# Two FFN gate-up passes: the weight sums of the block-product down are gathered in steps 2 to 7 of each group, and the small tables move to the four-tile part

## The chip, the cores and the metric

The kernel runs on one core of one Trainium2 chip. The metric is the device time of one execution in microseconds (us), the median of several runs. Beside it stands one execution that the hardware profiler recorded: its span (first to last instruction) and its trace. TensorE multiplies, VectorE (DVE) and ScalarE (ACT) do elementwise work, GpSimd (POOL) and SyncE (SP) mostly issue DMA transfers.

## The reference, cut to what matters

The input is 1,024 prompt rows and 128 sample rows of width 1,024, so nine tiles of 128 rows, through one layer: a SwiGLU feed-forward block, a mixer (window attention and a spatial gate), and a second SwiGLU block, each between RMS norms. What the change touches is

```python
def swiglu(x, w_gate, w_up, w_down):
    return (jax.nn.silu(x @ w_gate) * (x @ w_up)) @ w_down
x = x + 0.5 * rms_norm(swiglu(rms_norm(x, norm_g[0]), f1_g, f1_u, f1_d), norm_g[1])
...
x = x + 0.5 * rms_norm(swiglu(rms_norm(x, norm_g[4]), f2_g, f2_u, f2_d), norm_g[5])
```

with an inner width of 2,816, all in float32. The relative-bias table and the attention sinks, which the small tables below come from, are used only in the mixer.

## The kernel before, in words

**Exact products from halves.** Every operand is split into a rounded part and a rest (`hi` and `lo`; `wh`, `wl` for weights): ScalarE copies the rounded part (L158), VectorE subtracts (L161, "rest-cut" below). A product is three matmuls, `mm3`, at L306 to L308; the third is the first to need `wl`.

**Tiles and parts.** The nine row tiles are worked in two parts, five tiles (`parts1[0]`, then `parts2[0]` in the second block) and four tiles (`parts1[1]`, `parts2[1]`). Each part has a gate-up pass and a down pass. So the order is: five-tile gate-up, five-tile down, four-tile gate-up, four-tile down; the mixer; and the same four passes again.

**A gate-up pass** has eleven groups of 256 weight columns (`NG`). In a group the product is formed by seven block products instead of eight, in the order A11, S1, S2, S4, S3, A12, A22, for gate and up each. That makes fourteen steps; `drive` counts them through the whole pass and runs, before step i, the tasks listed under i. The first group of the first pass is plain and has 16 steps. The weight blocks S1 to S4 are sums that VectorE forms from raw weights (L200). In the rows S1 is `arena<-wr`, S2 `gn<-arena,wr`, S4 `arena<-wr,gn` and S3 `wr<-wr`. Behind the products VectorE adds results (L600) and multiplies gate by up (L658).

**The weight loads.** The raw weights lie in three buffers `wr`. A group takes two, raw 0 and raw 1, each of two transfers (gate and up, 512 KB each) that SP issues at L140. `fetch` issues the next load as soon as the buffer it needs is free. The buffer that the next group's raw 1 goes to is that of this group's raw 0, free when the rest-cut of S3 is done. The next group's S1 needs raw 1.

**The weight sums.** The five-tile down pass also uses block products, and four of its right-hand blocks (T1 to T4) are sums of the down weights. `down_sums` makes them during the five-tile gate-up: for each of eleven row blocks f, POOL loads two pieces of 512 KB into one of two places of `arena` (L232), VectorE does four subtractions of 128x512 (L239, "sums"), and POOL stores 1 MB to `t_d` (L241). A load into a place waits for the store out of it. `spread` places a task every so many steps; `in_order` ties its first ScalarE and VectorE instruction behind what was emitted before it on that engine. What is not tied, a scheduler places.

**The small tables.** `small_loads` clears five tiles on VectorE (L926) and loads tables with some twenty tiny transfers on POOL; two of them bring the sinks to `sink_p`, eight to `sink_s`. `small_turns` multiplies the bias table out on TensorE, negates the sinks on VectorE (`nsink_p`, `nsink_s`, L949), writes the bias spread `rb`, 1 MB, from POOL (L950), and turns a small weight matrix.

Of the kernel before, what the change touches and what calls it, by code (L numbers as in the profile page):

```python
# [32 lines left out]
NG = D_FF // 256  # L33
# [9 lines left out]
def tile_hybrid_layer(  # L43
# [38 lines left out]
    def tmp(n=BW):  # L82
        return fslot(F32, n)
# [40 lines left out]
    raws = {"n": 3}  # L124
# [118 lines left out]
        return ([lambda: load(0)] + [lambda f=f, i=i: make(f, i) for f in range(NG - 1) for i in range(4)] +  # L243
                [lambda: load(NG - 1)], [lambda i=i: make(NG - 1, i) for i in range(4)])

    def spread_sums(up, w_d, t_d, i):

        most, rest = down_sums(w_d, t_d)
        spread(up, most, i, (107 - i) / len(most))
        spread(up, rest, 114, 2)  # L250

    def plan_down(w_d, t_d):
        for _, right, _ in DOWN:
# [395 lines left out]
    def gate_up(part):  # L649

        w, gate = part.w, {}

        def done(g, m, c, j, v, in_place):
            if m == 0:
                t = gate[c, j] = v if in_place else tmp(w)
                nc.scalar.activation(out=t, in_=v, func=AF.Silu)  # L656
            else:
                nc.vector.tensor_tensor(out=part.g[2 * g + c][:, j * w:(j + 1) * w], in0=gate[c, j], in1=v,  # L658
                                        op=ALU.mult)

        return block_products(part, [part.order(g) for g in range(NG)], [2] * NG, done)
# [195 lines left out]
    def drive(gen, tasks):  # L857

        i = 0
        while True:  # L860
            for t in tasks.pop(i, ()):
                t()
            if next(gen, gen) is gen:
                break
            i += 1
        assert not tasks, sorted(tasks)

    def in_order(task):

        def f():  # L870
            seen = nc.cur_bb.bb.instructions
            n = len(seen)
            task()
            for eng in (mybir.EngineType.Activation, mybir.EngineType.DVE):
                mine = [i for i in seen[n:] if i.engine == eng]
                before = next((i for i in reversed(seen[:n]) if i.engine == eng), None)
                if mine and before is not None:
                    tc.add_manual_dep(mine[0], before.name, mybir.DependencyInfo(
                        mybir.DependencyClass.NoSync, mybir.DependencyReason.DATA), reason="in_order")
        return f  # L880

    def strict(task, engines=(mybir.EngineType.PE, mybir.EngineType.Activation, mybir.EngineType.DVE)):

        seen = nc.cur_bb.bb.instructions
        n = len(seen)
        task()
        for eng in engines:
            before = next((i for i in reversed(seen[:n]) if i.engine == eng), None)
            for i in [i for i in seen[n:] if i.engine == eng]:
                if before is not None:  # L890
                    tc.add_manual_dep(i, before.name, mybir.DependencyInfo(
                        mybir.DependencyClass.NoSync, mybir.DependencyReason.DATA), reason="strict")
                before = i

    def spread(tasks, todo, i, step):

        for t in todo:
            tasks.setdefault(int(i), []).append(in_order(t))
            i += step
# [59 lines left out]
    parts1 = [Part(TILES[0], 0, 5, True), Part(TILES[1], 0, 4)]  # L959
# [4 lines left out]
    t1_d, t2_d = (dram.tile([P, NG, 4, 512], F32, name=f"t{i}_d") for i in (1, 2))  # L964
# [78 lines left out]
    def next_tasks(part, src):  # L1043


        def begin():
            raws["n"] = 2

        def load():
            t = wr.tile([P, 2048], F32, tag="wr", name="wr")  # L1050
            for i, v in enumerate((place(0), gnp.tile([P, D], F32, tag="gn", name="gn"), t[:, :D], t[:, D:])):
                part.load(src, i, v)

        def end():
            raws["n"] = 3

        up, dn = {14 * (NG - 1) + (2 if src is x_in else 0): [begin]}, {90: [load]}
        n = norm_tasks(part.tiles, part.h)
        spread(dn, n[:part.n + 1], 103, 1.2)
        spread(dn, n[part.n + 1:], 111, 2)  # L1060
        spread(dn, part.operand_tasks()[0] + [end], 121, 4.4)
        return up, dn


    up, dn = next_tasks(parts1[1], x_in)
# [8 lines left out]
    up[2] = [lambda t=t: strict(t) for t in norm_tasks([3, 4], part.h, True, [nc.scalar, nc.vector])]  # L1074
    for i, t in zip((10, 11, 12, 13, 14, 16, 17, 19), part.sums()):
        up.setdefault(i, []).append(t)
    up.setdefault(14, []).append(lambda: strict(small_loads))
    spread(up, [small_turns], 45, 1)
    spread_sums(up, f1_d[0], t1_d, 15)
    drive(gate_up(parts1[0]), up)  # L1080
    drive(down_blocks(parts1[0]), dn)


    drive(gate_up(parts1[1]), {14 * (NG - 1): [lambda: raws.update(n=2)]})

# [700 lines left out]
    up, dn = next_tasks(parts2[1], x2_d)  # L1788
    spread(up, late, 0, 1.5)
    spread(up, [x2_inverse] + [lambda i=i: x2_put_last(i) for i in (3, 0, 1, 2)], 7, 2)  # L1790
    spread_sums(up, f2_d[0], t2_d, 22)
    drive(gate_up(parts2[0]), up)
    drive(down_blocks(parts2[0]), dn)

# [81 lines left out]
```

## Time and profile before

| what | us |
|---|---|
| median of 3 runs (lowest to highest) | 2560.33 (2557.41 to 2561.31) |
| the profiled execution | 2564.02 |
| its span | 2562.3 |
| PE busy | 2507.5 (98%) |
| DVE busy | 1996.2 (78%) |
| ACT busy | 1425.5 (56%) |
| mean granted clock of TensorE | 0.993 of full speed |

The profiled execution lies 3.69 us above the median. Some 55 us of the span are not covered by PE. A change of the order in which VectorE works can pay only in such gaps, in the time in which TensorE had the lower clock, or not at all. "A group" in the rows below is the time from one point of the pass to the same point of the next group: the moment at which the last S4 product is ready and VectorE adds it (called the mark).

### The profile page before, as it was taken

Reading aid. Unit: us, or ns where it says so; the run is one execution under the profiler, and the core shown is the slowest. Engines: PE = TensorE matmul, PEld = TensorE weight load, DVE = VectorE, ACT = ScalarE, POOL = GpSimd, SP = SyncE. Lnnn points to the kernel's source line nnn. Section 1 sums busy time; section 2 is a strip of 40 time slices with the busy share of each in tenths; the row PEclk is TensorE's granted clock in tenths of the full one; section 3 lists DMA queues with packets and bytes.
Section 4 is the critical chain, followed back from the end, with each engine's and each line's share of the span. In section 5 each row is a group of like instructions: output and inputs, shape, how many; then the busy total and the mean of one; then the engine's idle time right before and its main releaser. Section 6 shows DMA issues by size and latency. Waiting matters only on the chain.

```text
span 2562.3 us, 43644 instructions
## 1 busy us (share of the span) xinstructions
PE 2507.5 (98%) x16848; PEld 2352.5 (92%) x16848; DVE 1996.2 (78%) x3508; ACT 1425.5 (56%) x2692; POOL 236.8 (9%) x372
## 2 busy tenths in 40 slices
PE   9989999999999999999999999999999999999998
PEld 8989987999978999999989899997999987899986
DVE  7778777888877686787857877787887786888885
ACT  6434457555565555776446568646444456655552
POOL 1100000000110000011400101140001000000030
PEclk9999999999999999999999999999999999999999
DMA  5764344533443224424533344373566335533362
GB/s 157 203 209 158 105 158 161 164 115 116 144 165 105 83 79 137 146 78 146 181 111 93 128 149 128 98 257 103 181 214 213 121 126 173 178 116 116 125 205 83
DMA packets 243856, 366.89 MB, mean 143 GB/s; under 512 B 13640, under 2 KB 181040, under 8 KB 240832
## 3 DMA queue, kind: packets, MB, share of 16 engines
q1 hardware_dynamic: 192048, 229.66, 28.0%
q0 software_dynamic: 29344, 110.29, 13.1%
q10 hardware_dynamic: 22256, 24.15, 2.7%
q8 instruction: 132, 2.16, 0.4%
q14 instruction: 76, 0.62, 0.1%
HBM read 300.81 MB, written 63.18 MB: 142 GB/s over the span
## 4 chain that ended last, share of the span: by engine, by line
PE 81%; DVE 8%; DMA 6%; ACT 3%; issue 2%; ACTq 0%; POOL 0%; SPq 0%; DVEq 0%; POOLq 0%
PE ps L308 25%; PE ps L306 25%; PE ps L307 25%; DMA wr<-in_ffn_w_up_dram 3%; DVE wl L161 2%; PE ps L1486 2%; PE ps L487 1%; PE ps L1473 1%; PE ps L1438 1%; DVE arena L239 1%; ACT wh L158 1%; DMA wr<-in_w_in_dram 1%; DVE arena_r L317 0%; PE ps L1285 0%; DMA sink_p<-in_attn_sinks_dram 0%
## 5 line engine op out<-in xcount | busy, mean ns | idle before, releaser
L306 PE MATMUL ps<-arena_r,wh 128*128 128x320 f32 (+1 forms) x4160 | 1242.2, 299 | 15.7 <-DVE t L600 9.3
L308 PE MATMUL ps<-arena_r,wl 128*128 128x320 f32 (+1 forms) x4160 | 1228.6, 296 | 13.1 <-DVE wl L161 12.8
L307 PE MATMUL ps<-arena_r,wh 128*128 128x320 f32 (+1 forms) x4160 | 1228.9, 296 | 0.5 <-DVE arena_r L317 0.3
L306 PEld LDWEIGHTS ps<-arena_r,wh 128*128 128x128 f32 x4160 | 786.5, 189 | 19.8 <-issue 11.0
L308 PEld LDWEIGHTS ps<-arena_r,wl 128*128 128x128 f32 x4160 | 785.5, 189 | 17.1 <-DVE wl L161 16.8
L307 PEld LDWEIGHTS ps<-arena_r,wh 128*128 128x128 f32 x4160 | 787.0, 189 | 1.9 <-DVE arena_r L317 1.1
L161 DVE TENSOR_TENSOR wl<-wr,wh 128x1024 fp32r<-128x1024 f32 (+1 forms) x444 | 544.7, 1228 | 219.8 <-ACT wh L158 216.9
L158 ACT CAST wh<-wr 128x1024 fp32r<-128x1024 f32 (+1 forms) x444 | 455.2, 1026 | 210.2 <-PE ps L307 147.4
L306 PE MATMUL ps<-wh,arena_r 128*128 128x512 f32 x892 | 358.6, 402 | 2.9 <-ACT arena_r L316 2.9
L308 PE MATMUL ps<-wh,arena_r 128*128 128x512 f32 x892 | 353.9, 398 | 1.8 <-DVE arena_r L317 1.8
L307 PE MATMUL ps<-wl,arena_r 128*128 128x512 f32 x892 | 352.5, 395 | 1.3 <-DVE wl L161 1.3
L316 ACT CAST arena_r<-arena 128x512 fp32r<-128x512 f32 (+4 forms) x280 | 155.2, 567 | 187.3 <-PE ps L307 136.9
L317 DVE TENSOR_TENSOR arena_r<-arena,arena_r 128x512 fp32r<-128x512 f32 (+4 forms) x280 | 176.4, 647 | 55.6 <-ACT arena_r L316 52.0
L308 PEld LDWEIGHTS ps<-wh,arena_r 128*128 128x128 f32 x892 | 167.6, 188 | 44.1 <-DVE arena_r L317 3.9
L306 PEld LDWEIGHTS ps<-wh,arena_r 128*128 128x128 f32 x892 | 168.0, 188 | 42.7 <-ACT arena_r L316 5.0
L307 PEld LDWEIGHTS ps<-wl,arena_r 128*128 128x128 f32 x892 | 168.1, 188 | 40.5 <-DVE wl L161 2.0
L158 ACT CAST wh<-arena 128x1024 fp32r<-128x1024 f32 (+1 forms) x130 | 134.6, 1035 | 124.5 <-PE ps L307 67.1
L600 DVE TENSOR_TENSOR t<-t,ps 128x320 f32<-128x320 f32 (+1 forms) x384 | 169.1, 447 | 41.2 <-PE ps L308 31.3
L604 ACT COPY t<-ps 128x320 f32<-128x320 f32 (+1 forms) x384 | 149.3, 395 | 77.1 <-PE ps L308 73.4
L161 DVE TENSOR_TENSOR wl<-arena,wh 128x1024 fp32r<-128x1024 f32 (+1 forms) x130 | 156.4, 1203 | 29.8 <-ACT wh L158 29.4
L656 ACT ACTIVATE t<-t 128x256 f32<-128x256 f32 (+1 forms) x129 | 57.2, 444 | 213.3 <-DVE t L600 213.1
L200 DVE TENSOR_TENSOR arena<-wr 128x1024 f32<-128x1024 f32 (+1 forms) x65 | 78.4, 1206 | 69.3 <-DMA wr<-in_ffn_w_up_dram 51.5
(287 smaller groups left out, 2363.7 us busy)
## 6 DMA issues: line engine op xcount, KB each, us to landing
wr<-in_ffn_w_gate_dram SPq DMA_DIRECT2D x88, 512.0 KB, 4.1
wr<-in_ffn_w_up_dram SPq DMA_DIRECT2D x88, 512.0 KB, 5.1
wr<-in_w_in_dram SPq DMA_DIRECT2D x84, 512.0 KB, 5.1
wr<-in_ffn_w_down_dram SPq DMA_DIRECT2D x32, 1024.0 KB, 5.1
arena<-in_ffn_w_down_dram POOLq DMA_DIRECT2D x44, 512.0 KB, 4.8
t_d<-arena POOLq DMA_DIRECT2D x22, 1024.0 KB, 5.0
wr<-t_d SPq DMA_DIRECT2D x16, 1024.0 KB, 5.1
arena<-x POOLq DMA_DIRECT2D x19, 512.0 KB, 4.6
```

Source lines behind the costliest of these rows:

```text
L158: nc.scalar.copy(out=self.hi, in_=self.src)
L161: nc.vector.tensor_tensor(out=self.lo, in0=self.src, in1=self.hi.bitcast(F32), op=ALU.subtract)
L200: nc.vector.tensor_tensor(out=out, in0=x, in1=y, op=op)
L306: nc.tensor.matmul(out, lh, rh, start=start, stop=False, skip_group_check=again)
L307: nc.tensor.matmul(out, lh, rl, start=False, stop=False, skip_group_check=again)
L308: nc.tensor.matmul(out, ll, rh, start=False, stop=stop, skip_group_check=again)
L316: nc.scalar.copy(out=hi, in_=src)
L317: nc.vector.tensor_tensor(out=lo, in0=src, in1=hi.bitcast(F32), op=ALU.subtract)
L600: nc.vector.tensor_tensor(out=out, in0=a, in1=b, op=ALU.add)
L604: nc.scalar.copy(out=t, in_=ps)
L656: nc.scalar.activation(out=t, in_=v, func=AF.Silu)
L1486: nc.tensor.matmul(po[:, c0:c0 + P], self.vz[:, at:at + P], pt[:, a, :].rearrange("p (c t) -> p c t", c=2)[:, :, 64 * e:64 * e + 64], star ...
```

## The change: what it does

Three things. The sums are no longer spread evenly over the steps (every 2.19 steps from step 15 in the first block, every 2.02 from step 22 in the second). Those of the first ten row blocks stand, six to a group, at steps `14 * group + 2` to `14 * group + 7` of groups 1 to 6, and the last four of them in group 7, with the load of the eleventh block behind. The four sums of that block follow from step 114. The first load stands at step 15 in both blocks. The small tables leave the five-tile gate-up of the first block: `small_loads` moves to step 16 of the four-tile gate-up, `small_turns` to step 47 there; its two VectorE copies (L953, L960) come to stand right behind the rest-cut of S3 of that group, and the store of `rb` behind them. All arithmetic stays.

```diff
--- before.py
+++ after.py
@@ -243,11 +243,17 @@
         return ([lambda: load(0)] + [lambda f=f, i=i: make(f, i) for f in range(NG - 1) for i in range(4)] +
                 [lambda: load(NG - 1)], [lambda i=i: make(NG - 1, i) for i in range(4)])
 
-    def spread_sums(up, w_d, t_d, i):
+    def spread_sums(up, w_d, t_d):
+
 
         most, rest = down_sums(w_d, t_d)
-        spread(up, most, i, (107 - i) / len(most))
-        spread(up, rest, 114, 2)
+        up.setdefault(15, []).append(in_order(most.pop(0)))
+        load_last = most.pop()
+        for i, t in enumerate(most):
+            n = 14 * (1 + i // 6) + 2 + i % 6
+            up.setdefault(n, []).append(in_order(t))
+        up.setdefault(n + 1, []).append(in_order(load_last))
+        spread(up, rest, 14 * 8 + 2, 1.5)
 
     def plan_down(w_d, t_d):
         for _, right, _ in DOWN:
@@ -1074,14 +1080,14 @@
     up[2] = [lambda t=t: strict(t) for t in norm_tasks([3, 4], part.h, True, [nc.scalar, nc.vector])]
     for i, t in zip((10, 11, 12, 13, 14, 16, 17, 19), part.sums()):
         up.setdefault(i, []).append(t)
-    up.setdefault(14, []).append(lambda: strict(small_loads))
-    spread(up, [small_turns], 45, 1)
-    spread_sums(up, f1_d[0], t1_d, 15)
+    spread_sums(up, f1_d[0], t1_d)
     drive(gate_up(parts1[0]), up)
     drive(down_blocks(parts1[0]), dn)
 
 
-    drive(gate_up(parts1[1]), {14 * (NG - 1): [lambda: raws.update(n=2)]})
+    up = {14 * (NG - 1): [lambda: raws.update(n=2)], 16: [lambda: strict(small_loads)]}
+    spread(up, [small_turns], 47, 1)
+    drive(gate_up(parts1[1]), up)
 
 
 
@@ -1788,7 +1794,7 @@
     up, dn = next_tasks(parts2[1], x2_d)
     spread(up, late, 0, 1.5)
     spread(up, [x2_inverse] + [lambda i=i: x2_put_last(i) for i in (3, 0, 1, 2)], 7, 2)
-    spread_sums(up, f2_d[0], t2_d, 22)
+    spread_sums(up, f2_d[0], t2_d)
     drive(gate_up(parts2[0]), up)
     drive(down_blocks(parts2[0]), dn)
 
```

Three places show how instructions move. Line numbers from L248 on are six higher in the changed kernel, so L600 there is L606.

VectorE in the second block's five-tile gate-up, one group from the forming of S4 to that of the next S1, before (`wl` is a rest-cut, L239 a sum):

```order
L200 TENSOR_TENSOR arena<-wr,gn 128x1024
L239 TENSOR_TENSOR arena<-arena 128x512
L161 TENSOR_TENSOR wl<-gn,wh 128x1024
L239 TENSOR_TENSOR arena<-arena 128x512
L200 TENSOR_TENSOR wr<-wr 128x8x128
L161 TENSOR_TENSOR wl<-arena,wh 128x1024
L239 TENSOR_TENSOR arena<-arena 128x512
L161 TENSOR_TENSOR wl<-wr,wh 128x1024 x2
L600 TENSOR_TENSOR t<-t,ps 128x320 x2
L200 TENSOR_TENSOR arena<-wr 128x1024
```

The same piece after the change, from the group's first sum, which stands behind the rest-cut of S1, to the next S1:

```order
L239 TENSOR_TENSOR arena<-arena 128x512
L664 TENSOR_TENSOR arena<-t,ps 128x320
L200 TENSOR_TENSOR arena<-wr,gn 128x1024
L161 TENSOR_TENSOR wl<-gn,wh 128x1024
L239 TENSOR_TENSOR arena<-arena 128x512 x2
L161 TENSOR_TENSOR wl<-arena,wh 128x1024
L239 TENSOR_TENSOR arena<-arena 128x512 x2
L161 TENSOR_TENSOR wl<-wr,wh 128x1024 x2
L606 TENSOR_TENSOR t<-t,ps 128x320
L239 TENSOR_TENSOR arena<-arena 128x512
L606 TENSOR_TENSOR t<-t,ps 128x320
L200 TENSOR_TENSOR arena<-wr 128x1024
```

Before, seven sums stand between S1 and the rest-cut of S3 (the first of the two `wl<-wr` in one row), one of them ahead of the first rest-cut behind S1. After, five stand there, all behind the third rest-cut, and the sixth stands behind the rest-cut of S3. In the first block's five-tile gate-up the new order is the same but for all six sums standing ahead of the rest-cut of S3.

VectorE in the four-tile gate-up of the first block after the change, from the clearing of the sink tiles to the rest-cut of A22; before, the rows L932 and L955 were not there:

```order
L932 MEMSET sink_p 128x8
L932 MEMSET sink_s 128x2
L932 MEMSET w 128x4
L161 TENSOR_TENSOR wl<-arena,wh 128x1024
L323 TENSOR_TENSOR arena_r<-arena,arena_r 128x512 x2
L161 TENSOR_TENSOR wl<-wr,wh 128x1024
L955 TENSOR_SCALAR nsink_p<-sink_p 128x8
L161 TENSOR_TENSOR wl<-wr,wh 128x1024
L606 TENSOR_TENSOR t<-t,ps 128x256 x2
L664 TENSOR_TENSOR arena<-t 128x256
L955 TENSOR_SCALAR nsink_s<-sink_s 128x2
L161 TENSOR_TENSOR wl<-wr,wh 128x1024
```

The clearing of `sink_p`, its loads on POOL and its use in `nsink_p` now stand within one group; before there was more than a group between them. `nsink_p` stands ahead of the rest-cut of A12, `nsink_s` ahead of that of A22.

POOL in the first five-tile gate-up, loads and stores of the sums after the first, before and then after:

```order
L241 DMA t_d<-arena 128x2048
L232 DMA arena<-in_ffn_w_down_dram 128x1024 x2
L241 DMA t_d<-arena 128x2048
L232 DMA arena<-in_ffn_w_down_dram 128x1024 x2
L950 DMA rb<-t 1024x1x256
L241 DMA t_d<-arena 128x2048 x2
L232 DMA arena<-in_ffn_w_down_dram 128x1024 x4
L241 DMA t_d<-arena 128x2048
```

```order
L241 DMA t_d<-arena 128x2048
L232 DMA arena<-in_ffn_w_down_dram 128x1024 x2
L241 DMA t_d<-arena 128x2048 x2
L232 DMA arena<-in_ffn_w_down_dram 128x1024 x4
L241 DMA t_d<-arena 128x2048
L232 DMA arena<-in_ffn_w_down_dram 128x1024 x2
```

Before, a load mostly stands behind each store, with `rb` among them. After, every second time two stores are issued one behind the other and four loads follow. In the second block the queue mostly keeps its order of one store, then two loads.

## Rows read from the trace of the kernel before

**Rows 1.** The page, parts 1 and 5: busy time by engine; one of the costliest groups.

```profile
PE 2507.5 (98%) x16848; PEld 2352.5 (92%) x16848; DVE 1996.2 (78%) x3508; ACT 1425.5 (56%) x2692; POOL 236.8 (9%) x372
...
L600 DVE TENSOR_TENSOR t<-t,ps 128x320 f32<-128x320 f32 (+1 forms) x384 | 169.1, 447 | 41.2 <-PE ps L308 31.3
```

**Rows 2.** Three groups, first five-tile gate-up: length, busy by engine, clock, DMA.

```profile
120.58:154.70 34.12, 27.09 (x170) 26.45 (x169) 19.27 (x25) 11.12 (x18) 2.64 (x5) 0.90 0.67 208
154.70:184.18 29.48, 26.69 (x170) 26.20 (x169) 22.35 (x31) 11.35 (x18) 3.16 (x6) 0.94 0.55 196
208.82:233.46 24.64, 24.64 (x170) 24.64 (x169) 19.28 (x26) 11.13 (x18) 2.04 (x4) 1.00 0.51 184
```

**Rows 3.** The same view, eight groups of the second five-tile gate-up.

```profile
1957.86:1984.42 26.56, 25.16 (x170) 24.66 (x169) 20.48 (x28) 10.81 (x18) 2.14 (x4) 1.00 0.56 197
...
sum 203.39, PE 199.16 PEld 197.17 DVE 161.25 ACT 87.78 POOL 15.37; mean PE 24.90 PEld 24.65 DVE 20.16 ACT 10.97 POOL 1.92
```

**Rows 4.** VectorE timeline, second five-tile gate-up: start, duration, line [idle before].

```profile
1936.37 1.23 DVE L200 TENSOR_TENSOR arena<-wr 128x1024 f32<-128x1024 f32 x1 [4.11 <-DMA wr<-in_ffn_w_up_dram]
...
1953.43 0.68 DVE L239 TENSOR_TENSOR arena<-arena 128x512 f32<-128x512 f32 x1
1954.03 2.45 DVE L161 TENSOR_TENSOR wl<-wr,wh 128x1024 fp32r<-128x1024 f32 x2
...
1962.92 1.23 DVE L200 TENSOR_TENSOR arena<-wr 128x1024 f32<-128x1024 f32 x1 [4.57 <-DMA wr<-in_ffn_w_up_dram]
...
2034.70 1.23 DVE L200 TENSOR_TENSOR arena<-wr 128x1024 f32<-128x1024 f32 x1 [0.52 <-DMA wr<-in_ffn_w_up_dram]
```

**Rows 5.** Timeline of the SP queue, same stretch: issues of the weight loads.

```profile
1955.27 0.37 SPq L140 DMA_DIRECT2D wr<-in_ffn_w_gate_dram  x1
...
2029.10 0.37 SPq L140 DMA_DIRECT2D wr<-in_ffn_w_gate_dram  x1
```

**Rows 6.** Timeline of the POOL queue, same stretch.

```profile
1954.88 1.05 POOL L232 DMA_DIRECT2D arena<-in_ffn_w_down_dram  x2 [4.55 <-DMA t_d<-arena]
```

**Rows 7.** Timeline of the POOL queue, first five-tile gate-up.

```profile
56.44 1.39 POOL L931 DMA_DIRECT2D sink_p<-in_attn_sinks_dram  x2
...
64.44 0.50 POOL L934 DMA_DIRECT2D sink_s<-in_attn_sinks_dram  x1 [3.61 <-DMA sink_p<-in_attn_sinks_dram]
69.25 0.50 POOL L934 DMA_DIRECT2D sink_s<-in_attn_sinks_dram  x1 [4.30 <-DMA sink_p<-in_attn_sinks_dram]
...
111.62 0.78 POOL L950 DMA_DIRECT2D rb<-t  x1 [0.67 <-DVE t L947]
116.29 0.54 POOL L241 DMA_DIRECT2D t_d<-arena  x1 [3.89 <-DVE arena L239]
```

**Rows 8.** Timeline of the SP queue, first five-tile gate-up.

```profile
117.16 0.37 SPq L140 DMA_DIRECT2D wr<-in_ffn_w_gate_dram  x1
```

**Rows 9.** Timeline of VectorE, first five-tile gate-up.

```profile
55.36 0.07 DVE L926 MEMSET sink_p<- 128x8 f32 x1
...
90.20 0.16 DVE L949 TENSOR_SCALAR nsink_p<-sink_p 128x8 f32<-128x8 f32 x1
...
131.60 1.22 DVE L200 TENSOR_TENSOR arena<-wr 128x1024 f32<-128x1024 f32 x1 [10.54 <-DMA wr<-in_ffn_w_up_dram]
```

**Rows 10.** The chain that ended last, first five-tile gate-up: start, us, what.

```profile
69.25 4.99 DMA sink_s<-in_attn_sinks_dram
```

**Rows 11.** Timeline of VectorE, four-tile gate-up.

```profile
488.31 1.28 DVE L317 TENSOR_TENSOR arena_r<-arena,arena_r 128x512 fp32r<-128x512 f32 x2
489.61 1.23 DVE L161 TENSOR_TENSOR wl<-wr,wh 128x1024 fp32r<-128x1024 f32 x1
492.43 1.23 DVE L161 TENSOR_TENSOR wl<-wr,wh 128x1024 fp32r<-128x1024 f32 x1 [1.60 <-ACT wh L158]
...
494.31 0.42 DVE L600 TENSOR_TENSOR t<-t,ps 128x256 f32<-128x256 f32 x1 [0.32 <-PE ps L308]
```

**Rows 12.** Busy time by stretch, one group of the four-tile gate-up.

```profile
494.31:514.02 19.71, 19.71 (x171) 19.71 (x170) 16.95 (x23) 11.13 (x19) 0.00 (x0) 1.00 0.36 108
```

## The prediction

> **What bounds the kernel now.** I read the page first: PE is busy 2507.5 of 2562.3 us [rows 1]. No shorter VectorE work can pay as such; only the some 55 us without PE and the time at the lower clock can. So the next view was busy time by group, to see which groups are longer than PE needs. An undisturbed group of the five-tile gate-up takes 24.64 us with PE busy throughout [rows 2]. In the first block two groups take 34.12 and 29.48 us [rows 2]: 9.48 and 4.84 us too long, 14.3 together. In them PE is idle for 7.03 and 2.79 us, and busy 2.45 and 2.05 us longer than 24.64 for as many matmuls, at a granted clock of 0.90 and 0.94 of full speed. In the second block eight groups take 203.39 us [rows 3] where 8 x 24.64 = 197.1: 6.3 us too long. These 20.6 us are all that the sums' new order can give back.
>
> What makes a group long is seen on VectorE and the queues. One group of the second block: VectorE forms S1 at 1936.37 [rows 4], the next raw 1 is issued at 1955.27 [rows 5], right behind the rest-cut of S3 [rows 4], and the next S1 waits for it until 1962.92 [rows 4]. So the group is a loop of two legs: VectorE's 18.90 us from S1 to the issue (seven sums among them), and 7.65 us of transfer. Together 26.55 us, which is the measured length of such a group, 26.56 [rows 3]; PE alone would take 24.64. A late S1 costs nothing at once: when VectorE comes to it PE still has S3 and A12 to do, 2 x 3.52 = 7.0 us, and the rest-cut of A22 behind S1 needs about 3.3 (1.2 for S1, two adds of 0.45 [rows 1], 1.2). So up to 3.7 us of wait are free, once; a loop longer than 24.64 uses them up and then costs its excess in every group.
>
> **The change part by part.** Per sum VectorE takes 0.60 us from start to start (1953.43 to 1954.03 [rows 4]).
>
> *Second block.* Of the seven sums in the VectorE leg five stay: 18.90 - 1.20 = 17.7 us. The transfer leg: 7.65 us with a load of 1 MB issued beside it [rows 6], 5.60 us without one (2029.10 [rows 5] to 2034.70 [rows 4]). The sums now come in one burst ahead of the issue, so a store or a load falls beside it in nearly every group: I take 7.65. 17.7 + 7.65 = 25.35, 0.7 over PE's pace, 5 groups x 0.7 = 3.5, less a good part of the free wait: 2.0 us stay of 6.3. Gain 4.3; bounds 1.5 (a leg of 8.5) and 6.3 (5.60).
>
> *First block, five-tile gate-up.* Six sums all stay ahead of the issue: 18.90 - 0.60 = 18.3 us. POOL now has in every second group a store, then a second store and a load, all about the time of the issue; in the others one store and a load. For the latter 7.65. For the former the trace has one row with more than one transfer beside it: the issue at 117.16 [rows 8], with `rb` from 111.62 and a store from 116.29 [rows 7], was waited for until 131.60 [rows 9], 14.4 us. `rb` is gone from here, so I take 10.5, a little nearer to 7.65. Two groups then take 2 x 18.3 + 10.5 + 7.65 = 54.75, 5.5 over 49.28; three such pairs 16.5, less the free 3.7 and about 0.5 for the short last group: some 12 us stay of 14.3. Gain 2; bounds 10 (7.65 everywhere: 6 x 1.3 - 3.7 = 4 stay) and -10 (14.4: about 24 stay). The matmuls and copies of `small_turns` go and come again elsewhere: 0.
>
> *Small tables in the four-tile gate-up.* Before, the sink tiles were cleared at 55.36 and negated at 90.20 [rows 9], when all had landed: no wait. The eighth sink load could be issued at 69.25, when the second `sink_p` load had landed [rows 7], 13.9 us after the clearing, and landed 4.99 us later [rows 10]. Now `nsink_p` comes right behind the rest-cut of S3. Placed on the old times of that group: two cuts start at 488.31 behind a rest-cut, so the clearing ends near 487.7 with 0.5 us of memsets added; the rest-cut of S3 ends at 489.61 + 1.23 + 0.5 = 491.3 [rows 11]; `sink_p` has landed at 487.7 + 13.9 - 1.0 = 500.6 (the first two table loads are issued earlier, about 1.0). VectorE waits 9.3 us. Behind it stands the rest-cut of A12: it was done at 493.66, now at 502.0. PE has one product, 19.71 / 7 = 2.82 us [rows 12], from the mark at 494.31 [rows 11], and its first two matmuls of A12: it stands from 497.4 to 502.0, 4.6 us. Then `nsink_s` waits for the eighth sink load, 500.6 + 5.0 = 505.6; the rest-cut of A22 ends near 507.1, PE wants it at 504.7: 2.4 us. The next rest-cuts follow tightly, about 0.7. Sum 7.7, and about 2 for the lower clock, as the two disturbed groups show it [rows 2]. Cost 10. Bounds: 3, if both loads land as the first did (64.44 - 56.44 = 8.0 us [rows 7]; then only A22 is late); 14, if raw 1, issued at the same time, holds the tiny loads up.
>
> *`rb`.* Issued right behind a raw 1, where there was nothing beside it. That leg goes from about 5.6 to 7.65 or more, and in that group the rest-cut of A22 stands behind S1. Cost 2; bounds 0 (the free wait takes it) and 4.
>
> Sum: 4.3 + 2 - 10 - 2 = -5.7, slower. The profiled execution would take 2564.02 + 5.7 = 2569.7; it lies 3.7 above the median, so the predicted median is 2560.3 + 5.7 = 2566. Less than 0.2%, some 5 us, can hardly be told from no change here.
>
> **A rule against a row.** The row at 117.16 says that a raw 1 waits for all that stands beside it, 14.4 us [rows 7 to 9]. The Trainium skill, "DMA: Bandwidth & Descriptors", section "Queues, rings and completion order", says that each DMA engine takes the queue rows with work in turn, a packet from each. By that all POOL transfers together could at most about double the moving time of raw 1, whose transfer comes on SP's row: a leg of some 9 us. The 14.4 us row speaks against it, the 7.65 us row agrees.
>
> **The rivals.**
>
> *A cap on the transfer leg.* If a raw 1 alternates with whatever POOL has queued, its leg is about 5.60 plus as much again without the start, near 9. Then two groups take 2 x 18.3 + 9 + 7.65 = 53.25, 4.0 over; three pairs less 3.7 and 0.5: 8 stay, gain 6 in place of 2: 2562. That is the rule above.
>
> *The first block heals wholly (faster).* Its two long groups had nine sums, four of them between S1 and the next rest-cut, and `rb`; both are gone, and the undisturbed group [rows 2] had sums in it too. Then nothing of the 14.3 stays: 4.3 + 14.3 - 10 - 2 = 6.6 gained, 2554. It decides if raw 1 lands within 24.64 - 18.3 = 6.3 us. Against it: with one transfer beside it it took 7.65.
>
> *The tables are not waited for.* If the sinks land before VectorE comes to `nsink_p`, within 4 us of the clearing, the 10 us go: 2556. Against it: 13.9 us in the one trace there is.
>
> *Stores and loads pile up.* If every second raw 1 takes 14.4 us, the first block loses 10 more than now: 4.3 - 10 - 10 - 2 = -17.7, 2578. For it speaks the new order on POOL, against it that `rb` is away.
>
> **How the numbers follow.** The forecast, 0.38, with a range of its own of 2560 to 2572, lies on both sides of the 5 us: 0.24 slower, 0.14 same. The cap 0.15: 0.12 same, 0.02 slower, 0.01 faster. The healing 0.20: 0.17 faster, 0.03 same. No table wait 0.10: 0.07 same, 0.03 faster. The pile 0.17: slower. In all 0.21 faster, 0.36 same, 0.43 slower. The range of 2553 to 2578 leaves the better half of the healing with small table costs out and the upper half of the pile.
>
> **What would show it.** In the second block, eight groups of about 199 us in place of 203.4, and S1 waiting as now but no rest-cut ahead of PE. In the first, groups that are alternately near 24.6 and some 3 to 5 us longer. In the four-tile gate-up, VectorE idle for about 9 and 3 us ahead of L955, and PE waiting there 4 to 5 and 2 us for rest-cuts. Wrong would make it above all: a wait at `nsink_p` shorter than 4 us, or first-block groups all at 24.64.

## The result, and the profile after

| | median us (lowest to highest) | against before |
|---|---|---|
| before, four runs | 2560.82 (2557.41 to 2564.84) | |
| changed, four runs | 2580.77 (2576.17 to 2586.59) | 1.0074, 95% interval 1.0058 to 1.0089 |

The changed kernel is slower, by 15 to 23 us. Forecast were 2566 us and a range of 2553 to 2578: the side was right, the size was not. The profiled execution took 2576.17 us, span 2574.4, 12.1 us more than that of before.

PE has as much to do as before [rows 1]: of the 12.1 us its busy time takes 2.0, and the rest is time without it. The page, part 1:

```profile
PE 2509.5 (97%) x16848; PEld 2354.9 (91%) x16848; DVE 1996.9 (78%) x3508; ACT 1426.3 (55%) x2692; POOL 236.2 (9%) x372
```

**First five-tile gate-up.** Busy time by stretch, from mark to mark as in [rows 2] (length, busy by engine with instructions, granted clock, DMA share, GB/s):

```profile
97.24:130.86 33.62, 27.26 (x170) 26.63 (x169) 20.63 (x27) 11.11 (x18) 2.15 (x5) 0.90 0.53 182
130.86:155.50 24.64, 24.64 (x170) 24.64 (x169) 20.64 (x27) 11.13 (x18) 2.63 (x5) 1.00 0.54 189
155.50:187.96 32.46, 28.03 (x170) 27.39 (x169) 20.63 (x27) 11.12 (x18) 2.64 (x5) 0.89 0.54 189
187.96:212.60 24.64, 24.64 (x170) 24.64 (x169) 20.63 (x27) 11.24 (x18) 2.14 (x4) 1.00 0.55 193
212.60:239.71 27.11, 25.15 (x170) 24.66 (x169) 19.34 (x26) 10.92 (x18) 0.54 (x1) 1.00 0.42 139
```

Every second group is long. In a long one PE stands for up to 6.4 us and is then granted a lower clock (0.50 of full speed from 167 to 173 us, behind PE's standing from some 162 to 167): 28.03 us of work where a group needs 24.64. Over eight groups, this kernel and then the one before (one extra matmul group there is `small_turns`):

```profile
97.24:313.97 216.73, 203.98 (x1346) 201.89 (x1345) 155.51 (x201) 88.89 (x138) 12.20 (x23) 0.97 0.48 164
```

```profile
94.67:307.46 212.79, 202.97 (x1352) 201.02 (x1351) 156.87 (x206) 89.14 (x138) 13.49 (x25) 0.98 0.53 170
```

Eight undisturbed groups are 197.1, so 19.6 us are lost where 15.7 were; 1.1 of the 15.7 are the matmuls of `small_turns`. Of the 19.6, 12.7 are time in which PE stands (216.73 less 203.98) and 6.9 are work at the lower clock (203.98 less 197.1). Ahead of the first of them 2.57 more are lost (its mark stands at 97.24, before at 94.67).

Why every second group: the POOL queue, the SP queue and VectorE of the changed kernel, as [rows 7 to 9] show them of before:

```profile
147.06 0.54 POOL L241 DMA_DIRECT2D t_d<-arena  x1 [15.71 <-DVE arena L239]
150.86 0.54 POOL L241 DMA_DIRECT2D t_d<-arena  x1 [3.26 <-DVE arena L239]
151.48 1.06 POOL L232 DMA_DIRECT2D arena<-in_ffn_w_down_dram  x2
156.12 1.05 POOL L232 DMA_DIRECT2D arena<-in_ffn_w_down_dram  x2 [3.57 <-DMA t_d<-arena]
```

```profile
151.72 0.37 SPq L140 DMA_DIRECT2D wr<-in_ffn_w_gate_dram  x1
...
183.18 0.37 SPq L140 DMA_DIRECT2D wr<-in_ffn_w_gate_dram  x1
```

```profile
164.53 1.23 DVE L200 TENSOR_TENSOR arena<-wr 128x1024 f32<-128x1024 f32 x1 [8.53 <-DMA wr<-in_ffn_w_up_dram]
...
189.21 1.23 DVE L200 TENSOR_TENSOR arena<-wr 128x1024 f32<-128x1024 f32 x1 [0.76 <-DMA wr<-in_ffn_w_up_dram]
```

VectorE's leg is 183.18 - 164.53 = 18.65 us in the four loops that begin from 108 to 189 us; in the one before them it is 16.1, in the one behind, with four sums, 17.3. The transfer leg is 164.53 - 151.72 = 12.8 with two stores and two loads of 1 MB about the issue, and 189.21 - 183.18 = 6.0 with one of each. In order the six legs are 13.9, 6.2, 12.8, 6.0, 10.9 and 7.5 us. VectorE at the start and at the end of these six loops, the mark before the first S1 and the last S1:

```profile
71.68 0.48 DVE L606 TENSOR_TENSOR t<-t,ps 128x320 f32<-128x320 f32 x1
...
78.21 1.23 DVE L200 TENSOR_TENSOR arena<-wr 128x1024 f32<-128x1024 f32 x1 [2.75 <-DMA wr<-in_ffn_w_up_dram]
...
243.59 1.23 DVE L200 TENSOR_TENSOR arena<-wr 128x1024 f32<-128x1024 f32 x1 [3.40 <-DMA wr<-in_ffn_w_up_dram]
```

What passed in the second of the long ones, from the DMA view of 151.7 to 165 us (packets, MB, share of 16 engines):

```profile
q0 software_dynamic: 720, 3.15, 64.8%
q1 hardware_dynamic: 1056, 1.05, 23.0%
...
wr<-in_ffn_w_up_dram SPq DMA_DIRECT2D x1, 512.0 KB, 12.3
```

POOL's 3.15 MB went in packets of 4.4 KB, raw 1 in packets of 1.0 KB, and raw 1 landed last of all.

**Four-tile gate-up.** Busy time by stretch: two groups with the tables, the one with `small_turns` and the one behind `rb`; an undisturbed one is 19.71 [rows 12]:

```profile
481.04:529.57 48.53, 42.12 (x339) 41.79 (x338) 34.69 (x53) 22.25 (x38) 11.03 (x21) 0.93 0.42 81
529.57:550.40 20.83, 20.83 (x177) 20.28 (x176) 17.33 (x24) 10.50 (x18) 0.77 (x1) 1.00 0.46 146
550.40:570.11 19.71, 19.71 (x171) 19.71 (x170) 16.17 (x22) 10.61 (x18) 0.00 (x0) 1.00 0.71 142
```

48.53 + 20.83 are 10.2 us more than three times 19.71: 9.1 about the tables and 1.1 for the matmuls of `small_turns`. Behind `rb` nothing is lost. VectorE's and PE's timelines there:

```profile
508.97 0.17 DVE L955 TENSOR_SCALAR nsink_p<-sink_p 128x8 f32<-128x8 f32 x1 [11.47 <-DMA sink_p<-in_attn_sinks_dram]
...
513.04 0.17 DVE L955 TENSOR_SCALAR nsink_s<-sink_s 128x2 f32<-128x2 f32 x1 [1.49 <-DMA w<-in_gmlp_w_s_dram]
```

```profile
510.36 0.58 PE L314 MATMUL ps<-arena_r,wl 128*128 128x256 f32 x1 [6.41 <-DVE wl L161]
```

**Second five-tile gate-up.** Seven groups by stretch; the eight of [rows 3] were 6.3 us too long:

```profile
1870.27:2045.63 175.36, 173.01 (x1178) 172.49 (x1177) 137.43 (x179) 77.31 (x120) 12.10 (x23) 1.00 0.55 190
```

That is 2.9 us more than 7 x 24.64, all of it in the first of them, the only one in which PE stands. Gained: 3.4.

So the profiles differ by 6.5 us lost in the first part (3.9 + 2.6), 10.2 in the second, 3.4 gained in the third: 13.3, of which the rest of the kernel gave back 1.2.

### The profile page after: what moved, and what is told of

Read it like the earlier page. It is cut to its first block, busy times and chain, and to the rows that moved or that the text cites. A ratio compares the mean times of both kernels' runs of the same rounds, so it can differ in the third digit from the quotient of the medians.

```text
span 2574.4 us, 43668 instructions
## 1 busy us (share of the span) xinstructions
PE 2509.5 (97%) x16848; PEld 2354.9 (91%) x16848; DVE 1996.9 (78%) x3508; ACT 1426.3 (55%) x2692; POOL 236.2 (9%) x372
## 4 chain that ended last, share of the span: by engine, by line
PE 80%; DVE 8%; DMA 5%; issue 4%; ACT 3%; POOL 0%; ACTq 0%; SPq 0%; DVEq 0%; POOLq 0%
PE ps L314 24%; PE ps L312 24%; PE ps L313 24%; DVE wl L161 2%; DMA wr<-in_ffn_w_up_dram 2%; PE ps L1492 2%; PE ps L493 1%; PE ps L1479 1%; PE ps L1444 1%; ACT wh L158 1%; DVE arena L239 1%; DMA wr<-in_w_in_dram 1%; DVE arena_r L323 1%; DMA sink_p<-in_attn_sinks_dram 1%; PE ps L1291 1%
## 5 line engine op out<-in xcount | busy, mean ns | idle before, releaser
L312 PE MATMUL ps<-arena_r,wh 128*128 128x320 f32 (+1 forms) x4160 | 1243.4, 299 | 23.1 <-DVE t L606 13.5
L312 PEld LDWEIGHTS ps<-arena_r,wh 128*128 128x128 f32 x4160 | 787.7, 189 | 27.2 <-issue 12.8
L314 PEld LDWEIGHTS ps<-arena_r,wl 128*128 128x128 f32 x4160 | 786.7, 189 | 20.1 <-DVE wl L161 19.6
L606 DVE TENSOR_TENSOR t<-t,ps 128x320 f32<-128x320 f32 (+1 forms) x384 | 170.0, 448 | 39.1 <-PE ps L314 29.2
```

The lines of the kernel that those rows point to most:

```text
L312: nc.tensor.matmul(out, lh, rh, start=start, stop=False, skip_group_check=again)
L314: nc.tensor.matmul(out, ll, rh, start=False, stop=stop, skip_group_check=again)
L606: nc.vector.tensor_tensor(out=out, in0=a, in1=b, op=ALU.add)
```

## The experiments

Each kernel was timed against the one before on the same chip, in five rounds; the ratio with its 95% interval counts. Where a profile is quoted it is that of one execution.

### Which part costs what: tables_back, tables_only, second_only

```diff
# tables_back: the changed kernel, tables as before
+    up.setdefault(14, []).append(lambda: strict(small_loads))
+    spread(up, [small_turns], 45, 1)
     spread_sums(up, f1_d[0], t1_d)
...
-    up = {14 * (NG - 1): [lambda: raws.update(n=2)], 16: [lambda: strict(small_loads)]}
-    spread(up, [small_turns], 47, 1)
-    drive(gate_up(parts1[1]), up)
+    drive(gate_up(parts1[1]), {14 * (NG - 1): [lambda: raws.update(n=2)]})
# tables_only: the kernel before with the reverse of these lines
# second_only: the kernel before with
-    spread_sums(up, f2_d[0], t2_d, 22)
+    spread_sums(up, f2_d[0], t2_d)        # the changed kernel's order
```

> The sums' new order in both blocks, the small tables and rb where they were before. Theory (the two traces: the first block's new order costs 6.3 us, the tables' new place 10.4, the second block gives 3.5): the four-tile gate-up falls back to 19.71 us per group, no wait at nsink_p there; the time is some 10 us under that of the changed kernel, 2570 us, if rb in the five-tile gate-up finds a leg of raw 1 that is long anyway, and up to 9 us more, 2579, if rb adds a long leg of its own. Rival (the tables cost nothing that the sums would not have cost there): within 3 us of the changed kernel's 2580.8.

> The sums' old order in both blocks, the small tables and rb moved to the four-tile gate-up. Theory: VectorE waits some 11 us at nsink_p and PE's groups there are 10 us longer; in the five-tile gate-up the group that took 34.12 us with rb beside raw 1 takes 24.64 to 27, so 7 to 9.5 come back: 2562 to 2564 us, of which the tables' wait is +10. Rival (that long group comes from the nine sums in it and not from rb): it stays above 30 us, and the time is 2568 to 2571.

> The sums' new order in the second block alone; first block and tables as before. Theory: second-block gate-up 3.5 us shorter, 2557.3 us. Rival (the 3.5 us between the two profiles are their own scatter): 2560 to 2562 us.

| | median us | before | ratio |
|---|---|---|---|
| tables_back | 2571.36 | 2561.70 | 1.0030 (1.0020 to 1.0040) |
| tables_only | 2557.04 | 2561.70 | 0.9986 (0.9975 to 0.9996) |
| second_only | 2557.86 | 2561.70 | 0.9981 (0.9971 to 0.9991) |

The move of the tables by itself makes the kernel faster, and by more than its theory had (2562 to 2564), though the wait at `nsink_p` is there in it too (11.15 us in its trace). The gain is in the five-tile gate-up. Eight groups of tables_only by stretch:

```profile
94.52:292.99 198.47, 197.62 (x1346) 197.13 (x1345) 155.63 (x203) 88.59 (x138) 12.71 (x24) 1.00 0.51 175
```

1.3 us are lost, where the kernel before lost 15.7 with the same order of the sums. So 14.4 of those 15.7 us came with `rb` and the tables, 1.1 of them as matmuls. Whether the bunched sums of the two long groups [rows 2] had a part in it stays open: the kernel before has ten sums between the S1 at 158.53 us and the next issue, and here no loop has more than six, so the bunch went with the tables. With the new order and `rb` in one place (tables_back):

```profile
96.15:319.33 223.18, 205.12 (x1352) 201.92 (x1351) 156.22 (x203) 89.55 (x138) 12.95 (x24) 0.96 0.52 164
```

26.1 us are lost: `rb` and the tables add 6.5 to what the new order loses alone, not 14.4. The six legs are 13.7, 14.6, 11.1, 6.8, 9.8 and 7.5 us: `rb` falls beside a short leg (6.2 in the changed kernel) and makes it long, and of the long ones behind it two are 1.7 and 1.1 shorter. That accounts for 7.9 of the 10 to 15 us by which the parts do not add up in the medians: -4.7 (tables), -3.8 (second block) and, with the tables at the old place, +13.5 for the first block's sums (9.7 + 3.8) make +5, while the whole change makes +15 to +20. second_only is as its theory had it; in its trace eight groups of the second block take 198.49 us.

### What holds the four-tile gate-up: late_negation, tables_later, after_again

```diff
# late_negation: out of small_turns into a task of its own, one group later
+    def negate():
+        for n_, v_ in ((nsink_p, sink_p), (nsink_s, sink_s)):
+            nc.vector.tensor_scalar(out=n_, in0=v_, scalar1=-1.0, scalar2=None, op0=ALU.mult)
...
+    up.setdefault(61, []).append(lambda: strict(negate))
# tables_later: this, and
-    up = {14 * (NG - 1): [lambda: raws.update(n=2)], 16: [lambda: strict(small_loads)]}
+    up = {14 * (NG - 1): [lambda: raws.update(n=2)], 22: [lambda: strict(small_loads)]}
```

> The changed kernel with only the two negations of the sink tiles moved one group later, 14 steps, and held there in VectorE's order; loads, onehot product, rb and transposes stay. Theory (the 10.4 us come from VectorE standing at nsink_p with the rest-cuts behind it): no VectorE wait over 2 us at a negation, PE does not stand for a rest-cut there, 2580.8 - 10 = 2571 us. Rival (the loads beside raw 1 or the work of the tables themselves cost it): no more than 3 us come back, 2578 or more.

> The changed kernel itself, beside the others on one chip, because its four timed runs lay between 2576.2 and 2586.6 us while a kernel that differed from it by two late instructions had 2571.6. If the parts that the traces show (6.3 + 10.4 - 3.5) are all there is, some 2574 us; if there is a further cost that the one profile misses, 2580 us again.

> The changed kernel with small_loads six steps later (step 22 in place of 16), so that the tiny loads are issued some 8 us later, behind the landing of raw 1, and with the negations one group later. Theory (new: the tiny loads hold raw 1 up, 12.8 to 14 us to its landing in place of 5 to 6, and VectorE's wait at the negation only covered that): no S1 waits over 2 us in the four-tile gate-up, no negation waits, its groups take 19.7 us but for the five matmuls of small_turns (about 1.1), and 8 to 9 us come back against the changed kernel. Rival (raw 0, issued then, is held up instead and PE waits for its rest-cuts): the wait stays 5 us or more, 3 us or less come back.

| | median us | before | ratio |
|---|---|---|---|
| late_negation | 2571.59 | 2561.70 | 1.0042 (1.0028 to 1.0057) |
| after_again | 2577.89 | 2562.61 | 1.0058 (1.0038 to 1.0077) |
| tables_later | 2568.24 | 2562.61 | 1.0022 (1.0009 to 1.0035) |

The median of late_negation is what the theory of the wait asked for, 6 to 9 us under the changed kernel's two medians, though its interval overlaps that of after_again. The trace speaks for the rival, but it is that of the slowest of the six executions (2582.46, with the other five from 2570 to 2576). In it no negation waits, and PE stands as long as before. VectorE's S1 and PE's wait:

```profile
513.03 1.23 DVE L200 TENSOR_TENSOR arena<-wr 128x1024 f32<-128x1024 f32 x1 [8.66 <-DMA wr<-in_ffn_w_up_dram]
```

```profile
514.64 0.58 PE L312 MATMUL ps<-arena_r,wh 128*128 128x256 f32 x1 [5.99 <-DVE t L606]
```

Now raw 1 is late: issued at 498.47, it is there 14.6 us later. Its groups, by stretch:

```profile
482.00:501.71 19.71, 19.71 (x171) 19.71 (x170) 17.73 (x28) 11.54 (x20) 5.42 (x10) 1.00 0.43 79
501.71:530.17 28.46, 22.47 (x171) 22.26 (x170) 16.95 (x22) 11.09 (x19) 5.62 (x11) 0.88 0.46 102
```

48.17 us, against 48.53. In this execution the wait at `nsink_p` had covered a second one of the same length. In the changed kernel's own trace the gate and up transfers issued in that stretch took 12.8 and 13.8 us to land as well. How late raw 1 was in the five faster executions no trace shows; by the median, moving the negations gave back a part by itself. The DMA view of late_negation from 498.5 to 504.5 us, with raw 1 issued:

```profile
DMA packets 41, 0.00 MB, mean 1 GB/s; under 512 B 41, under 2 KB 41, under 8 KB 41
...
q0 software_dynamic: 41, 0.00, 103.5%
```

Only POOL's tiny packets move, and 103.5% of 16 engines over 6 us is 99 us of engine time for 41 packets, some 2.4 us each. Raw 1's own queue (q1) first moves after 504.5 us. In tables_later the tables are issued from 501.53, the S1's find their raw 1, and PE waits nowhere from 480 to 561 us:

```profile
500.27:520.21 19.94, 19.94 (x171) 19.94 (x170) 17.17 (x27) 11.24 (x19) 8.93 (x17) 1.00 0.72 108
520.21:541.27 21.06, 21.06 (x177) 20.50 (x176) 17.27 (x24) 10.39 (x18) 2.86 (x6) 1.00 0.41 119
```

Its theory holds: with the tiny loads behind raw 1's landing, and the negations later too, the 9 us are gone, 9.7 us between the medians of tables_later and after_again. How they divide between the late raw 1 and the wait at the negation is open. after_again, the changed kernel in another set of runs, confirms its time (1.0058) and its waits (groups of 49.70 us for 48.53).

### What makes the first block's groups long: no_transfers, wide_rows, short_rows

```diff
# no_transfers: the first block without loads and stores of the sums
-            for h in range(2):
+            for h in range(2 if t_d is not t1_d else 0):
...
-            if i == 3:
+            if i == 3 and t_d is not t1_d:
...
# wide_rows: the raw loads of groups 1 to 10 of the first five-tile gate-up, other weights of the same size
...
+        for j, r in enumerate(raw):
+            if wide_rows:
+                r.srcs = [w[wide_rows[2] + 512 * j:wide_rows[2] + 512 * j + P, 0:1024]
+                          .rearrange("p (k n) -> p k n", n=256) for w in wide_rows[:2]]
# short_rows: the first block's loads (and its stores likewise)
-                nc.gpsimd.dma_start(out=t[:, h], in_=w_d[r0:r0 + P, :])
+                for c in range(0, D, 256 if t_d is t1_d else D):
+                    e = c + (256 if t_d is t1_d else D)
+                    nc.gpsimd.dma_start(out=t[:, h, c:e], in_=w_d[r0:r0 + P, c:e])
```

> Leaves work out: the changed kernel without the loads of the down weights and the stores of their sums in the first block (the sums run on what stands in the arena, the down part reads plain weights in their place). VectorE's order is unchanged, six sums per group ahead of the issue. Theory (the first block's loss is the transfer leg: 13.9, 12.8 and 10.9 us beside two stores and a load): each leg 5.6 to 6.3 us, the loop 18.65 + 5.6 = 24.25, so groups of 24.64 us: 19.3 us less in the first gate-up, of which the 2 to 3 us of its first group, with PE waiting for casts that the sums hold up, stay. Rival (six sums in a bunch are too many for VectorE by themselves): groups above 27 us stay.

> Leaves the right weights out: in the first five-tile gate-up each raw load takes as many bytes from 128 whole stretches of 4 KB in place of 512 of 1 KB; the bytes of raw and POOL transfers, their order and VectorE's stay. In the changed kernel's slow leg POOL's queue moved 4.19 MB in 864 packets (4.85 KB each) while raw 1 had 1056 packets of 0.99 KB. Theory (the engines take a packet from each queue in turn, so raw 1 gets a fifth of POOL's bytes as long as POOL has any): with packets of 4 KB it gets nearly half, its leg in the even groups falls from 13.9, 12.8 and 10.9 to some 9 us, and 8 to 11 us come back against the changed kernel. Rival (bytes asked for earlier go first, or queues share by bytes): legs of 11 to 14 stay, no more than 3 us come back.

> The same from the other side: the changed kernel with POOL's loads and stores of the first block cut into strips with rows of 1 KB (8 loads of 128 KB for 2 of 512, 2 stores of 512 KB for 1 of 1 MB), same bytes. Theory (a packet in turn): raw 1 gets half, its even legs fall to some 8 to 9 us, 8 to 11 us come back. The strips take more time to issue on POOL, which moves some of the bytes to later; that alone could give 2 to 4 us. Rival (bytes in order): legs of 11 to 14 stay.

| | median us | before | ratio | eight groups, us |
|---|---|---|---|---|
| no_transfers | 2552.61 | 2562.61 | 0.9962 (0.9950 to 0.9974) | 197.12 |
| wide_rows | 2568.71 | 2560.16 | 1.0026 (1.0015 to 1.0038) | 206.94 |
| short_rows | 2560.99 | 2560.16 | 1.0001 (0.9991 to 1.0011) | 202.42 |

no_transfers settles the first question. Its VectorE does the same sums in the same bunches, and no group is long:

```profile
93.46:290.58 197.12, 197.12 (x1346) 197.12 (x1345) 156.36 (x201) 91.55 (x138) 0.67 (x1) 1.00 0.29 89
```

Without their transfers the sums cost the groups nothing, so all 19.6 us come with the transfers. (This kernel leaves the sums of the first block out of the down pass, which reads plain weights in their place.)

wide_rows asks how. The same bytes stand about the issue of raw 1 (DMA view, 147.7 to 159 us), in fewer packets of raw 1:

```profile
q0 software_dynamic: 712, 3.13, 74.1%
q1 hardware_dynamic: 288, 1.05, 23.1%
...
wr<-in_ffn_w_up_dram SPq DMA_DIRECT2D x1, 512.0 KB, 9.4
```

```profile
157.58 1.22 DVE L203 TENSOR_TENSOR arena<-wr 128x1024 f32<-128x1024 f32 x1 [6.56 <-DMA wr<-in_ffn_w_up_dram]
```

From its issue at 147.75 the leg is 9.8 us, where it was 12.8; the other long ones are 10.9 (13.9) and 10.0 (10.9). So the size of raw 1's packets counts: bytes in the order in which they were asked for would have left the legs as they were. Wide rows alone are not faster: with nothing beside it, the leg behind the issue at 275.39 is 6.2 us, and 6.4 in the changed kernel. The Trainium skill, "DMA: Bandwidth & Descriptors", section "Queues, rings and completion order", has the engines go round the queues a packet at a time. wide_rows agrees with it, if what the profile counts as packets are the page's. Its DMA view, 151.7 to 155.7 us, and then that of the changed kernel, 156.7 to 160.7:

```profile
q1 hardware_dynamic: 221, 0.84, 52.0%
q0 software_dynamic: 211, 0.80, 49.6%
```

```profile
q1 hardware_dynamic: 799, 0.80, 58.4%
q0 software_dynamic: 213, 0.74, 47.3%
```

In wide_rows the two queues move as many packets each. In the changed kernel raw 1 moves nearly four to POOL's one, about as many bytes, so there the turns are not seen packet by packet. Taken as a rule all the same, raw 1 gets 1.0 KB for each 4.4 KB of POOL's and ends about with POOL's 3.15 MB: 4.2 MB in 12.3 us, as measured. With packets of 3.64 KB raw 1 lets 1.05 x 4.4 / 3.64 = 1.27 MB of POOL's by; 2.3 MB at the 370 GB/s of wide_rows' window are 6.3 us, and with some 2.8 for the start of a leg (5.60 us alone [rows 4, 5] less 1.05 MB at the same rate) an estimate of 9.1, where 9.4 were measured. The same working gives 14.1 for the 12.3 of the changed kernel, so it is rough. The gain of 8 to 11 us is there (9.2 between the medians of wide_rows and after_again, which ran on two chips), the 9 us of the leg nearly. That the sizes count is shown; by which rule is argued.

short_rows gave more than its theory asked, and does not test it: POOL's packets became only little shorter (1.50 MB in 498 of them from 142.6 to 151 us, 3.0 KB each). What changed is that its many issues bring the bytes later, only 1.50 MB beside that raw 1, and its leg is 7.0 us. It agrees with the bytes beside raw 1 making the leg, without showing it.

### A better place for the sums: sums_in_leg, six_in_leg, leg_and_tables

```diff
# sums_in_leg
-            n = 14 * (1 + i // 6) + 2 + i % 6
+            n = 14 * (1 + i // 5) + 9
...
-        spread(up, rest, 14 * 8 + 2, 1.5)
+        spread(up, rest, 14 * 9 + 10, 0.5)
# six_in_leg
-            n = 14 * (1 + i // 6) + 2 + i % 6
+            n = 14 * (1 + i // 6) + 9
...
-        spread(up, rest, 14 * 8 + 2, 1.5)
+        spread(up, rest, 14 * 8 + 9, 0.5)
# leg_and_tables: six_in_leg and tables_later
```

> The changed kernel with five sums per group in place of six, all at step 9, which puts them in VectorE's order behind the rest-cuts of S3 and A12, in the time of raw 1's transfer where VectorE waits anyway. The leg from S1 to the issue falls from 18.65 by six sums of 0.6 to some 15 us, and the stores are issued behind raw 1, not ahead of it. Theory (the two legs make the loop): first-block groups at 24.64 us, 6 at most lost in all against 21.9 with the changed kernel: some 15 us faster than it, second-block gate-up 2 to 3 us shorter still. Rival (what POOL moves holds raw 1 up wherever it is issued, 13 us in every second group): the loop of 15 + 13 = 28 stays above 24.64 in every second group, and no more than 6 us come back.

> The changed kernel with its six sums per group all at step 9 in place of steps 2 to 7 (the last four likewise, at step 121), so that every sum is stored before the gate-up's outputs come to its place; tables as in the changed kernel. Theory (two legs; the sums' place decides, not their number per group): VectorE's leg some 15 us, groups of 24.64 us in both blocks, some 27 us faster than the changed kernel as with five per group, 2550 us. Rival (six per group bring a second store and a load into one leg): every second group stays above 26 us, 2556 us or more.

> six_in_leg and tables_later together. Theory (two separate costs that add up): 2577.9 - 27 - 9.7 = 2541 us, 0.8% under the kernel before, four-tile and five-tile gate-ups without a wait of PE over 1 us. Rival (with the five-tile part earlier, the tables meet another raw transfer): the four-tile group is still 5 us or more too long, 2546 us or more.

| | median us | before | ratio |
|---|---|---|---|
| sums_in_leg | 2550.49 | 2562.61 | 0.9952 (0.9934 to 0.9970) |
| six_in_leg | 2549.14 | 2560.16 | 0.9953 (0.9940 to 0.9966) |
| leg_and_tables | 2538.83 | 2560.16 | 0.9915 (0.9902 to 0.9929) |

In sums_in_leg the last sums of row blocks 8 and 10 run when outputs of the gate-up already stand in their place, so the down part gets other values there; the work is the same. six_in_leg has all of it in time. VectorE and the SP queue of six_in_leg:

```profile
98.61 1.22 DVE L200 TENSOR_TENSOR arena<-wr 128x1024 f32<-128x1024 f32 x1
...
115.99 1.41 DVE L239 TENSOR_TENSOR arena<-arena 128x512 f32<-128x512 f32 x2
...
123.25 1.22 DVE L200 TENSOR_TENSOR arena<-wr 128x1024 f32<-128x1024 f32 x1
```

```profile
112.18 0.37 SPq L140 DMA_DIRECT2D wr<-in_ffn_w_gate_dram  x1
```

VectorE's leg is 112.18 - 98.61 = 13.6 us. The sums fill the time in which it would wait, and in eight groups no S1 waits for raw 1. PE stands nowhere in eight groups of either block. sums_in_leg is 27 us faster than the changed kernel where its theory had 15; six_in_leg, at 2549 for 2550, has what its theory asked. Of six_in_leg and tables_later together, leg_and_tables (2538.8 for 2541), the two blocks' eight groups by stretch and the page's part 1:

```profile
92.49:289.61 197.12, 197.12 (x1346) 197.12 (x1345) 157.81 (x206) 91.69 (x138) 14.32 (x27) 1.00 0.53 185
...
1837.09:2034.21 197.12, 197.12 (x1346) 197.12 (x1345) 157.83 (x207) 90.48 (x137) 14.33 (x27) 1.00 0.53 185
```

```profile
PE 2502.2 (98%) x16848; PEld 2351.4 (93%) x16848; DVE 1995.7 (79%) x3508; ACT 1431.8 (56%) x2692; POOL 236.4 (9%) x372
```

It beats both kernels: 21 us less than before, some 40 less than the change.

## Why the prediction was wrong

| step | forecast | in the profiles |
|---|---|---|
| second block | +4.3 | +3.4 |
| first block, five-tile gate-up | +2 | -6.5 |
| small tables | -10 | -9.1, and 1.1 of matmuls that had left the first part |
| `rb` beside raw 1 | -2 | 0 |
| sum | -5.7 | -13.3 |

**The step that failed is the first block's term: the even transfer legs set at 10.5 us, and the 4.2 us taken off the loops.** Its form was right: two legs, a loop of two groups, every second raw 1 beside two stores and a load. The even legs, set at 10.5 "a little nearer to 7.65", were 13.9, 12.8 and 10.9. But the odd ones were 6.2, 6.0 and 7.5 for 7.65, and VectorE's leg was 16.1, four times 18.65, and 17.3 for 18.3 in all six. By luck these errors cancel: from the S1 at 78.21 to that at 243.59 the six loops took 165.4 us, 17.5 over six times 24.64, where 16.5 were forecast. What did not come are the 4.2 us taken off (3.7 of free wait, 0.5 for the last group). S1 stood 6.5 us behind its mark when the first of the loops began (71.68 to 78.21) and 3.9 behind it at the end of the sixth (239.71 to 243.59). So the free wait had been used up before, some of it was given back, and from mark to mark the six groups lost 20.2 us. In between, a PE that had stood and then worked at the lower clock was itself so late that the next S1 came only 2.2 and 1.3 us behind the mark. That the lower clock is why the free wait did not last is argued from these rows; no run tests it.

Also, 2.6 us were not costed at all: in the first groups VectorE still forms the operands, and sums put in there hold S-blocks up, so that PE waits for casts (4.3 us from 30 to 70 us, before 1.2; 3.7 in no_transfers, which has the sums there too). So 22.2 us stayed where 12 were forecast; and before, 15.7 were lost for the costed 14.3, the 1.1 of matmuls among them.

**The 14.4 us row was another case.** It was discounted because `rb` was gone, and the row has a reason of its own. The DMA view of the kernel before, 117 to 123 us, with raw 1 issued at 117.16:

```profile
DMA packets 143, 0.59 MB, mean 98 GB/s; under 512 B 1, under 2 KB 1, under 8 KB 142
...
q0 software_dynamic: 143, 0.59, 100.3%
```

For 6 us only POOL's packets move, 4.1 KB each, at 98 GB/s with all engines busy, and none of raw 1's. The changed kernel's leg became nearly as long in another way, with 3.15 MB of POOL's beside it at 315 GB/s in all. tables_only shows that the loss of before left with the tables and `rb`, 14.4 us of 15.7; the new order of the sums took some 21 (18.3 in the groups, 2.6 ahead). The rival "stores and loads pile up", with a chance of 0.17, had legs and loss nearly right, by a row that did not show its mechanism.

**The rule of the cap was read wrongly.** A turn of a packet each was taken as a turn of equal bytes, from which a leg of 9 us followed. The packets are not equal (1.0 KB against 4.4), and in wide_rows, where they nearly are, the leg of 12.8 became 9.8. The sizes are in the DMA view of before as well.

**The small tables.** The amount was right and the wait was where it was said, 11.5 us for 9.3, with PE standing 6.4 for 7.0 in two pieces. But the trace of late_negation shows that the mechanism named was not the only one: raw 1, issued in the same moments, was held up just as long in that execution. The upper bound had the two the wrong way round (raw 1 holding up the tiny loads).

**The second block** came as costed, 2.9 us left for 2.0. **`rb`** was at its lower bound.

What is left: the profiles differ by 12.1 us, the medians by 15.3 in one set of runs and 20 in the other. With 13 us on the 2560.3 the forecast's range would have held it. The profiled execution of before lies 3.2 us above the median of its four runs and that of the change 4.6 below its own, which is why the profiles show less. In which part of the kernel the other 2 to 7 us are was not found; runs of one kernel lie up to 15 us apart.

## What to carry to other kernels

Put work and its transfers into the time in which an engine waits for a load anyway, behind the issue of that load: the same six sums per group cost some 20 us ahead of the issue and nothing behind it. When a load is waited for, count what else is queued in bytes and in packets, since here a queue of short packets lost against one of long packets. And when a wait is found, ask what would end next without it: in the one trace of late_negation PE stood as long with the last wait removed.

## What was not expected of the hardware

- Loads of 4-byte pieces stopped a 1 MB load on another queue: for the first 6 us after its issue no packet of it moved, with tiny packets of some 2.4 us each in the engines; S1 had it after 14.6 us, where 5.6 were seen with nothing beside it [rows 4, 5].
- A load of 1 MB with the same transfers beside it was there 3 us earlier when its packets were 3.6 KB in place of 1.0.
- In the kernel before, POOL's packets of 4.1 KB filled all engines from 117 to 123 us at 98 GB/s, and no packet of the load issued at 117.16 moved; in the changed kernel 315 GB/s passed from 151.7 to 165 us. The slow packets are most likely those of `rb`, issued at 111.62 [rows 7]: a store's are larger (7.4 KB at 147 to 152 us in the changed kernel). No run has `rb` alone beside a raw 1.
- Undisturbed groups of the four-tile gate-up took 19.71 us in some executions and 19.94 in others, of the same kernel too (after, after_again), at a granted clock of 1.00 in both. Over eleven groups that is 2.5 us. Why stays open.
